# Moving blocks at a 1280-byte pitch, a shifted first weight tile, and smaller SSD buffers in an fp32 encoder kernel

## Chip, cores and metric

The kernel runs on one core of one Trainium2 chip. The metric is device time in microseconds (us) of one execution; several executions are timed and the median is quoted. One further execution is recorded by the hardware profiler, and all rows below come from that one.

## The reference, cut to what matters

Sixteen learned tokens are put ahead of 256 input tokens, so the sequence has L = 272 rows of D = 2048 channels. Layer 0 mixes tokens with a grouped 2-D Fourier transform, layer 1 with a bidirectional Mamba-2 mixer (SSD); each is followed by a SwiGLU channel mixer of width 5632. In layer 1 only the last 256 rows matter after the mixer.

```
h = concat(meta_tokens, x)                       # 272 x 2048
h = h + real(fft2(rms_norm(h))) @ fnet_w_out
h = h + (silu(u @ w_gate) * (u @ w_up)) @ w_down     # u = rms_norm(h)
h = h + ssd(rms_norm(h) @ w_in -> z, xBC, dt; conv of width 5 + silu on xBC) @ w_out
h = h + (silu(u @ w_gate) * (u @ w_up)) @ w_down
out = rms_norm(h)[16:]
```

## The kernel before, in words

All large products are taken as three fp32r matmuls, "high by high, high by low, low by high" (`mm3`, L108 to L110; the low part of the weights is L110). Every weight block comes from HBM as 1 MB in tile `w`; ScalarE rounds 1024 columns of it into `wh` (L101) and VectorE puts the rest into `wl` (L102), four buffers of each.

The stationary side of a matmul is 128 columns, 512 bytes a partition. The moving side is, in most products, a block of the normed input: `gh` (high) and `gl` (low) hold 16 blocks of 272 fp32 columns, and `gsl` picks block k. 272 columns are 1088 bytes, so block k begins 1088k bytes after the first: 64k bytes further each time if one counts modulo 256. `gh` itself begins at a multiple of 256, which a pad tile sees to. After the SSD mixer the same room is used as 16 blocks of 256 columns (`gh1`, `gl1`), 1024 bytes apart: each at a multiple of 256.

The helper `weights(..., place)` puts the split weights `place` elements into their buffer, whose size (4352 bytes) is a multiple of 256. The default is 16 elements, so the weights begin 64 bytes past a multiple of 256; `place` is 0 in the products in which the weights are the moving side, 512 columns wide (`w_z` in the SSD mixer and the down product of layer 1). There the stationary side is a slice of `gh` or of the hidden tile `hh`. `hh` and `hl` of layer 0 have blocks of 320 columns, 1280 bytes, of which 272 are used.

The order of the work is that of the program: in `swiglu` pieces of eight 128-column blocks of the hidden width; of each piece all gate and up products (`gemm_in`, 96 matmuls each, two PSUM tiles in turn), then the down product of the piece before. In layer 1 the pieces are 8, 8, 8, 8, 8, 2, 2 blocks: the gate and up products of the first two pieces stand one after the other (1536 matmuls, with `norm_scale` after the first 96), those of the later ones each follow a down product (768, 768, 768, 192, 192 matmuls).

In the SSD mixer eight head groups run through slots. A pair of groups begins with the B and the C products (`conv` on each, C with 258 columns that begin 56 bytes into a block), each group has two X products with `conv`, the `w_z` product, and then the output product of the group two back (`out_group`, L584; 48 matmuls for each of four q, moving side `yh`, `yl` at multiples of 256). `conv` is: L553 PSUM to `cu`, L559 ScalarE into `ca`, four L561 VectorE steps in `ca`, L563 SiLU into the destination. `to_tokens` transposes what `conv` made one slot later.

Two helpers are named in the steps below: `norm_scale` (one plain fp32 matmul, L172, then eleven VectorE steps into `rbc`) and `step_sizes` (the dt product and the decays).

Of the kernel before, what the change touches and what calls it, by code (L numbers as in the profile page):

```python
# [19 lines left out]
P = 128  # L20
D = 2048
# [19 lines left out]
XC, BC, CC = 0, DI, DI + G * NST  # L41
NRAW, NSP = 3, 4
RUN = 1024
LINE = 128
HC = 8
NEG = -1.0e30

# [2 lines left out]
def encoder(ctx: ExitStack, tc: tile.TileContext, I, out):  # L50
# [14 lines left out]
        return ptp.tile([P, 512], F32, tag="tp", name="tp")  # L65


    const.tile([P, LINE - 32], F32, name="pad")
    hT = const.tile([P, NB, L], F32, name="hT")
    gh = const.tile([P, NB, L], F32R, name="gh")  # L70
    gl = const.tile([P, NB, L], F32R, name="gl")
    ident = const.tile([P, P], F32, name="ident")
    ones = const.tile([P, P], F32, name="ones")
    cols = const.tile([P, 4 * P], F32, name="cols")

    def col(i):
        return cols[:, i : i + 1]
# [4 lines left out]
    def wffn(i, b):  # L82
        return col(32 + i * NB + b)

    def weights(src, k0, nk, c0, ncol, place=LINE // 8):

        w = wpool.tile([P, nk, ncol], F32, tag="w", name="w", bufs=NRAW)  # L90
        k1 = RUN // ncol
        nc.sync.dma_start(w.rearrange("p (u k) c -> p u (k c)", k=k1),
                          src[k0 // k1 : (k0 + nk) // k1, c0 // ncol].rearrange("u p x -> p u x"))
        parts = []
        n = min(nk, RUN // ncol)
        for k in range(0, nk, n):
            ks = slice(k, k + n)
            wh, wl = (wpool.tile([P, RUN + LINE // 2], F32R, tag=t, name=t, bufs=NSP)[:, place : place + n * ncol]
                      .rearrange("p (k c) -> p k c", c=ncol) for t in ("wh", "wl"))
            with tc.high_priority(offset=70):  # L100
                SC.copy(wh, w[:, ks, :])  # L101
                V.tensor_tensor(out=wl, in0=w[:, ks, :], in1=wh.bitcast(F32), op=ALU.subtract)  # L102
            parts.append((wh, wl))
        return parts
# [9 lines left out]
        return tuple(x[:, k % each, c0 : c0 + n] for x in u[k // each])  # L114


    gh1, gl1 = (x.rearrange("p b t -> p (b t)")[:, : NB * S].rearrange("p (b t) -> p b t", t=S) for x in (gh, gl))

    def gsl(k, a, b=L):
        if (a, b) == (NM, L):  # L120
            return gh1[:, k, :], gl1[:, k, :]
        return gh[:, k, a:b], gl[:, k, a:b]

    def gemm_in(src, c0, lo):

        n = L - lo
        pss = [mmtile(), mmtile()]
        for k0 in (0, 8):
            u = weights(src, k0, 8, c0, 256)
            for k in range(8):  # L130
                for j in range(2):
                    mm3(pss[j][:, :n], wsl(u, k, j * P), gsl(k0 + k, lo), k0 + k == 0, k0 + k == NB - 1)
        return pss
# [16 lines left out]
    ssq = npool.tile([P, L], F32, name="ssq")  # L150

    npool.tile([P, L], F32, tag="sq", name="sq", bufs=1)
    npool.tile([P, L], I32, tag="nyi", name="nyi")
    npool.tile([P, LINE // 2], F32, name="pad2")

    def norm_block(b, wcol, lo):

# [11 lines left out]
    def norm_scale(lo):  # L169

        ps = tptile()
        PE.matmul(ps[:, : L - lo], ones, ssq[:, lo:], start=True, stop=True)  # L172
        x = npool.tile([P, L], F32, tag="sq", name="nx", bufs=1)
        V.tensor_scalar(out=x[:, lo:], in0=ps[:, : L - lo], scalar1=1.0 / D, scalar2=EPS,
                        op0=ALU.mult, op1=ALU.add)
        yi = npool.tile([P, L], I32, tag="nyi", name="nyi")
        t = npool.tile([P, L], F32, tag="nyi", name="nt")
        y = rbc
        V.tensor_scalar(out=yi[:, lo:], in0=x[:, lo:].bitcast(I32), scalar1=1, scalar2=None,
                        op0=ALU.logical_shift_right)  # L180
        V.tensor_scalar(out=y[:, lo:].bitcast(I32), in0=yi[:, lo:], scalar1=-1.0, scalar2=float(0x5F3759DF),
                        op0=ALU.mult, op1=ALU.add)
        for it in range(3):
            V.tensor_tensor(out=t[:, lo:], in0=y[:, lo:], in1=y[:, lo:], op=ALU.mult)
            V.scalar_tensor_tensor(out=t[:, lo:], in0=t[:, lo:], scalar=-0.5, in1=x[:, lo:],
                                   op0=ALU.mult, op1=ALU.mult)
            V.scalar_tensor_tensor(out=y[:, lo:], in0=t[:, lo:], scalar=1.5, in1=y[:, lo:],
                                   op0=ALU.add, op1=ALU.mult)
# [4 lines left out]
    with ExitStack() as fx:  # L193
# [7 lines left out]
        ftl = early.tile([P, 2, 2, FD], F32R, name="ftl")  # L201
        fh = early.tile([P, NB, L], F32R, name="fh")
        fl = early.tile([P, NB, L], F32R, name="fl")
        tok = early.tile([P, 2, L], F32, name="tok")
        tokM = early.tile([KM, L], F32, name="tokM")
        tm3 = early.tile([KM, L], F32R, name="tm3")
        th = early.tile([P, 2, L], F32R, name="th")
        tl = early.tile([P, 2, L], F32R, name="tl")
# [12 lines left out]
        for q in range(4):  # L221
            nc.sync.dma_start(x[:, 1, q * 512 : (q + 1) * 512], xin[P : 2 * P, q * 512 : (q + 1) * 512])
        nc.sync.dma_start(rows, I["vectors"].rearrange("(i r) p -> r i p", r=P))
        nc.sync.dma_start(tok, I["c_tok"])
        nc.sync.dma_start(tokM, I["c_tokm"])
        nc.sync.dma_start(feat, I["c_feat"])

# [30 lines left out]

        def table(c, r):

            SC.activation(th[:, c, :], tok[:, c, :], AF.Identity, bias=0.0, scale=r)
            V.scalar_tensor_tensor(out=tl[:, c, :], in0=tok[:, c, :], scalar=r, in1=th[:, c, :].bitcast(F32),
                                   op0=ALU.mult, op1=ALU.subtract)

        with tc.manual_schedule():
# [8 lines left out]
            rA = rsqrt(early, ms3[:, 0:1], 1, "rA")  # L274
            residual(0, 0, pss[0])
            residual(0, 1, pss[1])
            SC.activation(gl.rearrange("p b t -> p (b t)")[:KM, :D], xm, AF.Square, accum_out=ssm[:KM])
            residual(0, 2, pss[2])
            residual(0, 3, pss[3])
            ps = mmtile()  # L280
# [16 lines left out]
            table(0, rA)  # L297
            rB = rsqrt(early, ms3[:, 1:3], 2, "rB")
            highM(quarters[0])
            SC.copy(cols, ps)  # L300
            residual(1, 2, pss[2])
            residual(1, 3, pss[3])
            table(1, rB[:, 0:1])
# [71 lines left out]
    def swiglu(layer, lo, tmp, pieces, down):  # L375
# [3 lines left out]
        for nf in pieces:  # L379

            hh = tmp.tile([P, HC, n + -n % 64], F32R, tag="hh", name="hh", bufs=2)[:, :, :n]
            hl = tmp.tile([P, HC, n + -n % 64], F32R, tag="hl", name="hl", bufs=2)[:, :, :n]
            for fp in range(nf // 2):
                c0 = (f0 + 2 * fp) * P
                s2 = []
                gate = gemm_in(wg, c0, lo)
                if c0 == 0:
                    norm_scale(lo)
                for ps in gate:
                    t1 = tmp.tile([P, n], F32, tag="t1", name="t1", bufs=2)  # L390
                    V.tensor_tensor(out=t1, in0=ps[:, :n], in1=rbc[:, lo:], op=ALU.mult)
                    s1 = tmp.tile([P, n], F32, tag="s1", name="s1", bufs=3)
                    SC.activation(s1, t1, AF.Silu)  # L393
                    GP.tensor_tensor(out=s1, in0=s1, in1=rbc[:, lo:], op=ALU.mult)  # L394
                    s2.append(s1)
                for j, ps in enumerate(gemm_in(wu, c0, lo)):
                    f = 2 * fp + j
                    t2 = tmp.tile([P, n], F32, tag="t2", name="t2", bufs=2)
                    V.tensor_tensor(out=t2, in0=ps[:, :n], in1=s2[j], op=ALU.mult)
                    SC.copy(hh[:, f, :], t2)  # L400
                    GP.tensor_tensor(out=hl[:, f, :], in0=t2, in1=hh[:, f, :].bitcast(F32), op=ALU.subtract)  # L401
            if pending is not None:
                down(*pending)
            pending = (f0, nf, hh, hl)
            f0 += nf
# [23 lines left out]
    with ExitStack() as fx:  # L429
# [2 lines left out]

        tm = sc0.tile([P, 5, P], F32, name="tm")
        tmM = sc0.tile([NM, H], F32, name="tmM")
        decA = sc0.tile([P, H], F32, name="decA")
        dsk = sc0.tile([P, H], F32, name="dsk")
        rtok = sc0.tile([P, 2 + 2 * 8], F32, name="rtok")[:, 0:2]
        scr = dram.tile([P, 2 * P], F32, name="scr")
# [28 lines left out]
        def step_sizes():  # L467
            u = weights(I["w_dt"], 0, NB, 0, P)
            ps = mmtile()
            for k in range(NB):  # L470
                mm3(ps[:, :L], wsl(u, k), gsl(k, 0), k == 0, k == NB - 1)
            norm_scale(0)


            pr = tptile()
            PE.matmul(pr[:, 0:1], ssq[:, CA[0] : CA[1]], ones[:, 0:1], start=True, stop=True)
            PE.matmul(pr[:, 1:2], ssq[:, CB[0] : CB[1]], ones[:, 0:1], start=True, stop=True)
            mst = sc0.tile([P, 2], F32, name="mst")
            V.tensor_scalar(out=mst, in0=pr[:, 0:2], scalar1=1.0 / D, scalar2=EPS, op0=ALU.mult, op1=ALU.add)
            rt = rsqrt(sc0, mst, 2, "rt")  # L480
# [68 lines left out]
        def conv(ps, blk, lo, dst):  # L549
# [1 line left out]
            n = L - lo  # L551
            u = so.tile([P, L], F32, tag="cu", name="cu", bufs=2)
            V.tensor_tensor(out=u[:, :n], in0=ps[:, :n], in1=rbc[:, lo:], op=ALU.mult)  # L553
            a = so.tile([P, L], F32, tag="ca", name="ca", bufs=2)

            def w(j):
                return col(114 + j * 48 + blk)
# [2 lines left out]
            for j, (o0, o1, i0) in ((0, (2, n, 0)), (1, (1, n, 0)), (3, (0, n - 1, 1)), (4, (0, n - 2, 2))):  # L560
                V.scalar_tensor_tensor(out=a[:, o0:o1], in0=u[:, i0 : i0 + o1 - o0], scalar=w(j),  # L561
                                       in1=a[:, o0:o1], op0=ALU.mult, op1=ALU.add)
            SC.activation(dst, a[:, :n], AF.Silu)  # L563

        def to_tokens(src, dst, dstM):

# [6 lines left out]

        def out_group(gi, q, yh, yl):

            u = weights(w_out, gi * 4, 4, q * 512, 512)
            for jp in range(2):
                pss = [mmtile(), mmtile()]
                for k in range(4):
# [145 lines left out]
        for gi in range(G):  # L725
            if gi % 2 == 0:

                bT = so.tile([P, 2, L], F32, tag="bT", name="bT", bufs=2)
                cT = so.tile([P, 2, S + 2], F32, tag="cT", name="cT", bufs=1)
                btok = sp.tile([P, 2, 2, P], F32, tag="btok", name="btok", bufs=2)  # L730
                btokM = sp.tile([NM, 2, P], F32, tag="btokM", name="btokM", bufs=2)
# [34 lines left out]
            pz = [mmtile(), mmtile()]  # L766
            for k in range(NB):
                if k % 4 == 0:
                    u = weights(I["w_z"], k, 4, gi * 512, 512, 0)
                for c, (a, b) in enumerate((CA, CB)):  # L770
                    mm3(pz[c], gsl(k, a, b), wsl(u, k % 4, 0, 512), k == 0, k == NB - 1)
            for c in range(2):
# [22 lines left out]
    with ExitStack() as fx:  # L795
# [2 lines left out]
        fw = tmp.tile([P, D], F32, name="fw")  # L798
        GP.dma_start(fw, I["norm_final_w"].partition_broadcast(P))
        sqj = tmp.tile([P, 512], F32, name="fsq")  # L800
        small = tmp.tile([P, LINE], F32, name="fsmall")
        sums = small[:, 0:8].rearrange("p (c q) -> p c q", c=2)
        ms = small[:, 8:10]

# [123 lines left out]
```

## Time and profile before

| what | us |
|---|---|
| median of three runs | 2446.23 (2445.91 to 2447.92) |
| the profiled execution, its own time | 2445.32 |
| its span, first to last instruction | 2443.5 |

The profiled execution is 0.9 us below the median. Matmuls overlap in the pipeline: each is listed with about 0.28 us, while the next one begins 0.113 to 0.125 us after it. The listed length is therefore not the cost; the step from start to start is. In a table of windows the count of a window also takes in the one to three matmuls that began ahead of it and still run at its left edge.

### The profile page before, as it was taken

The page shows a single profiled execution, that of the slowest core. Times are in us where ns is not written, and L with a number is a line of the kernel's source. Part 1 is how long each engine was busy: PE and PEld are TensorE (multiplying, and loading weights), DVE is VectorE, ACT ScalarE, POOL GpSimd, SP SyncE. Part 2 cuts the span into 40 slices and gives each one's busy share as a digit, 9 for nine tenths or more (in the row PEclk, how much of TensorE's full clock was granted, in tenths as well). Part 3 has the DMA queues.
Part 4 walks back from the last instruction along what each step waited for, and adds up shares of the span by engine and source line. Part 5 has one row for each costly group of instructions (what it writes and reads, how often), then busy time and mean ns, then how long its engine had stood idle before and what let it go on. Part 6 is the DMA issues. An engine that isn't in the chain of part 4 may idle for free.

```text
span 2443.5 us, 42924 instructions
## 1 busy us (share of the span) xinstructions
PE 2415.7 (99%) x17958; PEld 2305.0 (94%) x17958; DVE 1481.8 (61%) x2020; ACT 1212.1 (50%) x1784; POOL 407.6 (17%) x361
## 2 busy tenths in 40 slices
PE   8999999999999999999999999999999999999998
PEld 8999999999999999888989989989999998989887
DVE  7564544545454568778668768668554555555556
ACT  6444334343433346878557558445444443434334
POOL 3111111010101112231221221112221020202000
PEclk9999999999999999999999999999999999999999
DMA  5555555555555555655455555454655555555553
GB/s 165 175 177 180 175 173 175 181 179 174 174 179 181 175 173 175 216 174 189 164 179 193 180 173 184 162 173 161 202 191 186 191 184 192 184 194 184 190 192 132
DMA packets 115506, 438.66 MB, mean 180 GB/s; under 512 B 7360, under 2 KB 8080, under 8 KB 115136
## 3 DMA queue, kind: packets, MB, share of 16 engines
q1 hardware_dynamic: 110336, 417.86, 50.5%
q0 software_dynamic: 4832, 17.99, 2.3%
q8 instruction: 141, 2.31, 0.4%
q14 instruction: 53, 0.43, 0.0%
q10 hardware_dynamic: 144, 0.07, 0.0%
HBM read 433.66 MB, written 2.23 MB: 178 GB/s over the span
## 4 chain that ended last, share of the span: by engine, by line
PE 88%; DVE 4%; DMA 3%; issue 2%; ACT 2%; POOL 1%; SPq 0%; DVEq 0%; ACTq 0%; POOLq 0%
PE mm L109 28%; PE mm L110 28%; PE mm L108 28%; DMA pb<-scr 2%; DVE wl L102 1%; PE tp L659 1%; ACT wh L101 1%; DVE ca L561 1%; ACT pb L601 0%; DMA w<-fnet_w_out 0%; PE tp L643 0%; PE tp L682 0%; POOL pb L718 0%; PE tp L625 0%; PE tp L622 0%
## 5 line engine op out<-in xcount | busy, mean ns | idle before, releaser
L102 DVE TENSOR_TENSOR wl<-w,wh 128x1024 fp32r<-128x1024 f32 x786 | 971.1, 1237 | 833.3 <-ACT wh L101 830.2
L101 ACT CAST wh<-w 128x1024 fp32r<-128x1024 f32 x786 | 821.6, 1047 | 1085.6 <-PE mm L109 799.3
L109 PE MATMUL mm<-gl,wh 128*128 128x272 f32 (+2 forms) x3600 | 1027.0, 285 | 0.0
L110 PE MATMUL mm<-gh,wl 128*128 128x272 f32 (+2 forms) x3600 | 1024.3, 285 | 0.5 <-DVE wl L102 0.5
L108 PE MATMUL mm<-gh,wh 128*128 128x272 f32 (+2 forms) x3600 | 1021.8, 284 | 0.1
L109 PEld LDWEIGHTS mm<-gl,wh 128*128 128x128 f32 x3600 | 680.0, 189 | 0.8 <-issue 0.5
L108 PEld LDWEIGHTS mm<-gh,wh 128*128 128x128 f32 x3600 | 678.3, 188 | 1.1 <-issue 0.5
L110 PEld LDWEIGHTS mm<-gh,wl 128*128 128x128 f32 x3600 | 676.2, 188 | 0.9 <-DVE wl L102 0.7
L394 POOL TENSOR_TENSOR s<-s,rbc 128x272 f32<-128x272 f32 (+1 forms) x88 | 96.6, 1116 | 812.5 <-ACT s L393 812.5
L110 PE MATMUL mm<-hh,wl 128*128 128x272 f32 x704 | 201.8, 287 | 0.0
L109 PE MATMUL mm<-hl,wh 128*128 128x272 f32 x704 | 201.8, 287 | 0.0
L108 PE MATMUL mm<-hh,wh 128*128 128x272 f32 x704 | 201.8, 287 | 0.0
L401 POOL TENSOR_TENSOR hl<-t,hh 128x272 fp32r<-128x272 f32 (+1 forms) x88 | 97.0, 1120 | 395.4 <-ACT hh L400 395.4
L108 PE MATMUL mm<-yh,wh 128*128 128x256 f32 x512 | 145.5, 286 | 3.4 <-DVE hT L584 3.0
L109 PE MATMUL mm<-yl,wh 128*128 128x256 f32 x512 | 142.6, 279 | 0.5 <-DVE yl L688 0.5
L110 PE MATMUL mm<-yh,wl 128*128 128x256 f32 x512 | 142.5, 279 | 0.0
L108 PE MATMUL mm<-wh,hh 128*128 128x512 f32 x352 | 137.2, 390 | 0.0
L109 PE MATMUL mm<-wl,hh 128*128 128x512 f32 x352 | 137.1, 390 | 0.0
L110 PE MATMUL mm<-wh,hl 128*128 128x512 f32 x352 | 137.0, 389 | 0.0
L108 PEld LDWEIGHTS mm<-hh,wh 128*128 128x128 f32 x704 | 132.7, 188 | 0.0
L110 PEld LDWEIGHTS mm<-hh,wl 128*128 128x128 f32 x704 | 132.6, 188 | 0.0
L109 PEld LDWEIGHTS mm<-hl,wh 128*128 128x128 f32 x704 | 132.6, 188 | 0.0
(279 smaller groups left out, 2852.1 us busy)
## 6 DMA issues: line engine op xcount, KB each, us to landing
w<-ffn_w_gate SPq DMA_DIRECT2D x88, 1024.0 KB, 5.2
w<-ffn_w_up SPq DMA_DIRECT2D x88, 1024.0 KB, 5.1
w<-w_down SPq DMA_DIRECT2D x80, 1024.0 KB, 5.0
w<-w_xbc SPq DMA_DIRECT2D x48, 1024.0 KB, 5.3
w<-w_z SPq DMA_DIRECT2D x32, 1024.0 KB, 5.4
w<-ssd_w_out SPq DMA_DIRECT2D x32, 1024.0 KB, 5.0
w<-fnet_w_out SPq DMA_DIRECT2D x16, 1024.0 KB, 5.3
pb<-scr POOLq DMA_DIRECT2D x32, 512.0 KB, 5.6
```

Of the source, the lines that this page charges most:

```text
L101: SC.copy(wh, w[:, ks, :])
L102: V.tensor_tensor(out=wl, in0=w[:, ks, :], in1=wh.bitcast(F32), op=ALU.subtract)
L108: PE.matmul(ps, lhs[0], rhs[0], start=start, stop=False)
L109: PE.matmul(ps, lhs[0], rhs[1], start=False, stop=False)
L110: PE.matmul(ps, lhs[1], rhs[0], start=False, stop=stop)
L394: GP.tensor_tensor(out=s1, in0=s1, in1=rbc[:, lo:], op=ALU.mult)
L401: GP.tensor_tensor(out=hl[:, f, :], in0=t2, in1=hh[:, f, :].bitcast(F32), op=ALU.subtract)
L561: V.scalar_tensor_tensor(out=a[:, o0:o1], in0=u[:, i0 : i0 + o1 - o0], scalar=w(j), in1=a[:, o0:o1], op0=ALU.mult, op1=ALU.add)
L659: PE.matmul(py[:, e * HD : (e + 1) * HD], kern[c][:, e, :], xt[:, c, e * HD : (e + 1) * HD], start=True, stop=True)
```

## The change

Five things change. (1) `gh` and `gl` become one tile `g2` with blocks of 320 columns (`LP`), of which 272 are used; all 16 blocks begin at a multiple of 256 bytes. The 256-column form `gh1`, `gl1` stays packed at 1024 bytes, again at multiples of 256. Pads and tiles ahead of it are sized so that the starts of `g2`, `wh`, `wl`, the hidden tiles and the SSD tiles keep their place modulo 256. (2) The weights of `w_z` move from `place` 0 to 16. (3) A `first` argument: the first 1024-column part of the weights of some stretches of 256-column products begins at 0 instead of 64 bytes, which are the first gate product of every piece in layer 1 (24 matmuls) and the even q of `out_group` (the halves k = 0, 1 of its two column pairs). (4) `conv` works in place in its destination for the 272-column products; the C product keeps one `ca` buffer instead of two; `bT` has one buffer instead of two; `decA` lies in a free part of `tm`. (5) `norm_scale` uses `ssq` as its scratch, so the two small matmuls on `ssq` in `step_sizes` come ahead of it; the Fourier tables are loaded into `ssq`, the `sq` buffer and `rbc`, with two DMAs for `c_tok` instead of one; `cols` is 400 wide.

```diff
-LINE = 128
+LP = 320
+AT = 16
+NCOL = 400
...
-    gh = const.tile([P, NB, L], F32R, name="gh")
-    gl = const.tile([P, NB, L], F32R, name="gl")
+    g2 = const.tile([P, 2, NB, LP], F32R, name="g2")
+    gh, gl = g2[:, 0, :, :L], g2[:, 1, :, :L]
...
-    def weights(src, k0, nk, c0, ncol, place=LINE // 8):
+    def weights(src, k0, nk, c0, ncol, place=AT, first=None):
...
+            at = place if first is None or k else first
-            wh, wl = (wpool.tile([P, RUN + LINE // 2], F32R, tag=t, name=t, bufs=NSP)[:, place : place + n * ncol]
+            wh, wl = (wpool.tile([P, RUN + 64], F32R, tag=t, name=t, bufs=NSP)[:, at : at + n * ncol]
...
-    def gemm_in(src, c0, lo):
+    def gemm_in(src, c0, lo, first=AT):
-            u = weights(src, k0, 8, c0, 256)
+            u = weights(src, k0, 8, c0, 256, AT, None if k0 else first)
...
-        yi = npool.tile([P, L], I32, tag="nyi", name="nyi")
-        t = npool.tile([P, L], F32, tag="nyi", name="nt")
-        y = rbc
+        yi, t, y = ssq.bitcast(I32), ssq, rbc
...
-        nc.sync.dma_start(tok, I["c_tok"])
+        for c in range(2):
+            nc.sync.dma_start(tok[c], I["c_tok"][:, c])
...
-                gate = gemm_in(wg, c0, lo)
+                gate = gemm_in(wg, c0, lo, 0 if lo and fp == 0 else AT)
...
-        decA = sc0.tile([P, H], F32, name="decA")
+        decA = tm[:, 4, H:]
...
-            norm_scale(0)
             pr = tptile()
             PE.matmul(pr[:, 0:1], ssq[:, CA[0] : CA[1]], ones[:, 0:1], start=True, stop=True)
             PE.matmul(pr[:, 1:2], ssq[:, CB[0] : CB[1]], ones[:, 0:1], start=True, stop=True)
+            norm_scale(0)
...
-            a = so.tile([P, L], F32, tag="ca", name="ca", bufs=2)
+            a = dst if lo == 0 else so.tile([P, S + 2], F32, tag="ca", name="ca", bufs=1)
-            SC.activation(dst, a[:, :n], AF.Silu)
+            SC.activation(dst, a, AF.Silu)
...
-            u = weights(w_out, gi * 4, 4, q * 512, 512)
+            u = weights(w_out, gi * 4, 4, q * 512, 512, AT, None if q % 2 else 0)
...
-                bT = so.tile([P, 2, L], F32, tag="bT", name="bT", bufs=2)
+                bT = so.tile([P, 2, L], F32, tag="bT", name="bT", bufs=1)
...
-                    u = weights(I["w_z"], k, 4, gi * 512, 512, 0)
+                    u = weights(I["w_z"], k, 4, gi * 512, 512)
```

## Rows read from the trace of the kernel before

**Rows 1.** Page: the span, and the first line of busy time by engine.

```profile
span 2443.5 us, 42924 instructions
...
PE 2415.7 (99%) x17958; PEld 2305.0 (94%) x17958; DVE 1481.8 (61%) x2020; ACT 1212.1 (50%) x1784; POOL 407.6 (17%) x361
```

**Rows 2.** Waits of PE: what waited, for whom, us in total, times, longest.

```profile
PE tp L240 <- DMA ident<-c_ident: 5.2, 1, 5.2
PE mm L108 <- DVE hT L584: 3.0, 4, 1.2
```

**Rows 3.** Groups of PE's instructions, shapes kept apart: count, then busy us, mean ns.

```profile
L108 PE MATMUL mm<-gh,wh 128*128 128x272 f32 x2064 | 591.5, 287 | 0.0
L108 PE MATMUL mm<-gh,wh 128*128 128x256 f32 x1408 | 393.7, 280 | 0.1
...
L108 PE MATMUL mm<-yh,wh 128*128 128x256 f32 x512 | 145.5, 286 | 3.4 <-DVE hT L584 3.0 <-ACT yh L687 0.5
...
L108 PE MATMUL mm<-wh,gh 128*128 128x512 f32 x256 | 101.6, 397 | 0.0
...
L108 PE MATMUL mm<-gh,wh 128*128 128x258 f32 x128 | 36.6, 286 | 0.0
```

**Rows 4.** Windows of stretches: us, PE busy (matmuls), granted clock, DMA share, GB/s.

```profile
309.63:405.63 96.00, 96.00 (x770) 1.00 0.51 176
405.63:452.99 47.36, 47.36 (x386) 1.00 0.55 179
1720.00:1820.00 100.00, 100.00 (x885) 1.00 0.59 198
2010.39:2053.93 43.54, 43.54 (x194) 1.00 0.56 190
2053.93:2144.39 90.46, 90.46 (x770) 1.00 0.57 188
```

**Rows 5.** Windows inside two stretches of the output product (first, second of a group).

```profile
1347.00:1356.00 9.00, 9.00 (x82) 1.00 0.33 117
1361.00:1370.00 9.00, 9.00 (x79) 1.00 0.39 123
```

**Rows 6.** Timeline, PE, from a down product to the next gate product, layer 1.

```profile
2053.71 0.39 PE L110 MATMUL mm<-wh,hl 128*128 128x512 f32 x1
2053.93 0.28 PE L108 MATMUL mm<-gh,wh 128*128 128x256 f32 x1
2054.05 0.28 PE L109 MATMUL mm<-gl,wh 128*128 128x256 f32 x1
```

**Rows 7.** Timeline, PE, around the plain fp32 matmul of `norm_scale` in layer 1.

```profile
1708.70 0.60 PE L172 MATMUL tp<-ssq,ones 128*128 128x256 f32 x2
1708.94 0.47 PE L108 MATMUL mm<-gh,wh 128*128 128x256 f32 x1
```

**Rows 8.** Timeline, PE, beginning of a down product of layer 1.

```profile
2010.39 0.40 PE L108 MATMUL mm<-wh,hh 128*128 128x512 f32 x1
...
2011.55 0.39 PE L110 MATMUL mm<-wh,hl 128*128 128x512 f32 x1
...
2012.23 0.39 PE L110 MATMUL mm<-wh,hl 128*128 128x512 f32 x1
```

**Rows 9.** Timeline, PE: first matmul of a `w_z` product, first instruction behind it.

```profile
1323.18 0.48 PE L108 MATMUL mm<-wh,gh 128*128 128x512 f32 x1
...
1345.51 0.27 PE L568 MATMUL tp<-ident,xs 128*128 128x128 f32 x1
```

**Rows 10.** Groups of instructions, all engines, from 940 to 1700 us (SSD).

```profile
L561 DVE SCALAR_TENSOR_TENSOR ca<-cu,cols,ca 128x270 f32<-128x270 f32 (+3 forms) x192 | 86.4, 511 | 0.3 <-ACT ca L559 0.2
...
L563 ACT ACT_TABLE_LOAD x23 | 29.5, 1283 | 13.1 <-DVE ca L561 12.6
L559 ACT ACTIVATE ca<-cu,cols 128x272 f32<-128x272 f32 (+1 forms) x48 | 27.1, 606 | 11.3 <-DVE cu L553 11.2
```

**Rows 11.** The instructions that touch tile `tok`: the DMA issue.

```profile
L224 SPq DMA_DIRECT2D tok<-c_tok x1: 339/339/339, 9.8 to 9.8; - x1
```

More of the change, by code (lines that the diff above doesn't have):

```diff
@@ L65, in tptile @@
         return ptp.tile([P, 512], F32, tag="tp", name="tp")
-    const.tile([P, LINE - 32], F32, name="pad")
+    cols = const.tile([P, NCOL], F32, name="cols")
+    const.tile([P, 16], F32, name="pad")
     hT = const.tile([P, NB, L], F32, name="hT")
-    gh = const.tile([P, NB, L], F32R, name="gh")
-    gl = const.tile([P, NB, L], F32R, name="gl")
+    g2 = const.tile([P, 2, NB, LP], F32R, name="g2")
+    gh, gl = g2[:, 0, :, :L], g2[:, 1, :, :L]
     ident = const.tile([P, P], F32, name="ident")
     ones = const.tile([P, P], F32, name="ones")
-    cols = const.tile([P, 4 * P], F32, name="cols")
     def col(i):
@@ L114, in wsl @@
         return tuple(x[:, k % each, c0 : c0 + n] for x in u[k // each])
-    gh1, gl1 = (x.rearrange("p b t -> p (b t)")[:, : NB * S].rearrange("p (b t) -> p b t", t=S) for x in (gh, gl))
+    gh1, gl1 = (g2[:, i].rearrange("p b t -> p (b t)")[:, : NB * S].rearrange("p (b t) -> p b t", t=S)
+                for i in range(2))
     def gsl(k, a, b=L):
@@ L152, in encoder @@
     npool.tile([P, L], F32, tag="sq", name="sq", bufs=1)
-    npool.tile([P, L], I32, tag="nyi", name="nyi")
-    npool.tile([P, LINE // 2], F32, name="pad2")
+    npool.tile([P, 16], F32, name="pad")
     def norm_block(b, wcol, lo):
@@ L203, in encoder @@
         fl = early.tile([P, NB, L], F32R, name="fl")
-        tok = early.tile([P, 2, L], F32, name="tok")
-        tokM = early.tile([KM, L], F32, name="tokM")
+        tok = (ssq, npool.tile([P, L], F32, tag="sq", name="tok1", bufs=1))
+        tokM = rbc[:KM]
         tm3 = early.tile([KM, L], F32R, name="tm3")
@@ L259, in table @@
         def table(c, r):
-            SC.activation(th[:, c, :], tok[:, c, :], AF.Identity, bias=0.0, scale=r)
-            V.scalar_tensor_tensor(out=tl[:, c, :], in0=tok[:, c, :], scalar=r, in1=th[:, c, :].bitcast(F32),
+            SC.activation(th[:, c, :], tok[c], AF.Identity, bias=0.0, scale=r)
+            V.scalar_tensor_tensor(out=tl[:, c, :], in0=tok[c], scalar=r, in1=th[:, c, :].bitcast(F32),
                                    op0=ALU.mult, op1=ALU.subtract)
@@ L276, in encoder @@
             residual(0, 1, pss[1])
-            SC.activation(gl.rearrange("p b t -> p (b t)")[:KM, :D], xm, AF.Square, accum_out=ssm[:KM])
+            SC.activation(g2[:KM, 1].rearrange("p b t -> p (b t)")[:, :D], xm, AF.Square, accum_out=ssm[:KM])
             residual(0, 2, pss[2])
@@ L299, in encoder @@
             highM(quarters[0])
-            SC.copy(cols, ps)
+            SC.copy(cols, ps[:, :NCOL])
             residual(1, 2, pss[2])
@@ L800, in encoder @@
         sqj = tmp.tile([P, 512], F32, name="fsq")
-        small = tmp.tile([P, LINE], F32, name="fsmall")
+        small = tmp.tile([P, 128], F32, name="fsmall")
         sums = small[:, 0:8].rearrange("p (c q) -> p c q", c=2)
```

## The prediction, made before the changed kernel ran

> **What bounds the kernel now.** I read the page first: PE is busy for 99% of the span and its weight loads for 94%, while the next engine, DVE, is at 61% [rows 1]. Then the waits of PE, longest first after the start of the program: the costliest is 3.0 us in all, against 5.2 for the first load [rows 2]. So the time is the sum of PE's steps from one matmul to the next, and nothing that DVE, ACT or the DMAs save would be seen. The table of PE's instructions then says how many steps there are of each width [rows 3]; each row there is one of the three lines of `mm3`, so the counts go times three: 6192 matmuls of 272 columns on `gh`, 4224 of 256 on the packed form, 1536 of 256 on `yh`, 768 of 512 in `w_z`, 384 of 258. A mean of 276 to 290 ns in that table is not a step, because matmuls overlap. So the next view is that of windows that are cut at the first matmul of a stretch and the first behind it. Their length by the program's count of matmuls is the step, and here the kernel shows what the change is about: the same work goes at different steps, with the granted clock at 1.00 (the level of 2.4 GHz) in all of them [rows 4].
>
> - Gate and up of layer 0, blocks 1088 bytes apart, so that their starts move by 64 bytes modulo 256: 96.00 us by 768 matmuls, 125.0 ns.
> - Down of layer 0, the same 272 columns, the same weights at 64, but blocks 1280 bytes apart: 47.36 by 384, 123.3 ns.
> - Gate and up of layer 1, 256 columns: within the first long stretch 100.00 us hold 885 matmuls less the two or three that reach in from the left, 113.3 ns; in the stretch after a down product 90.46 by 768, 117.8 ns. The places of the operands are the same in both; only what came before differs.
> - The output products show the same two steps: windows of 9.00 us hold 82 or 79 [rows 5].
>
> The 256-column product thus has two patterns, a short step and a long step, and keeps the one in which it begins. Each of the five stretches that follow a down product has the long step; the long stretch before them has the short one, and it begins behind a plain fp32 matmul [rows 7].
>
> **The change part by part.** *Pitch of 1280 bytes.* After it, a 272-column product on `gh` has moving blocks at multiples of 256 and weights at 64: the arrangement of the down product of layer 0, down to the pitch. I take its step: 125.0 - 123.3 = 1.67 ns, times 6192 = **-10.3 us** [rows 3, 4]. The bounds are nothing and that. The 384 matmuls of C begin 56 bytes into a block before and after; no row has them with all blocks alike, so between nothing and the same 1.67 ns, 0.6 us; I take 0.
>
> *First weights at 0, gate products.* Of the 4224 gate and up matmuls of layer 1, the pieces behind a down product have 3 x 768 + 2 x 192 = 2688, all at 117.8. If the new beginning leaves them at the short step, that is 4.5 ns x 2688 = **-12.0 us** [rows 3, 4]. Is it likely? Where both operands begin at a multiple of 256, as in the down product of layer 1, the first five steps take 1.16 us (2010.39 to 2011.55), 232 ns each, and the next three 0.68, 227 each [rows 8], and the whole stretch averages 43.54 by 192, 226.8, twice 113.4 [rows 4]. So equal places pull a long-step beginning into the short step. The 24 matmuls with weights at 0 are four times as many as that took. What follows has the weights at 64, where a short step lasts for at least the 880 matmuls of its window. Against it stands the handover in [rows 6]: the down product has the short step (2053.71 to 2053.93, 0.22 us), the very next gate product with weights at 64 the long one at once (0.12). There the width changes together with the place; in the changed kernel the place alone changes, 24 matmuls on. I take that the short step survives it, by a small margin; the other end is nothing.
>
> *First weights at 0, output products.* Seven of the fourteen stretches of 96 and most of the last 288 have the long step, some 870 of 1536 matmuls; the short one in all of them would be -3.9 us [rows 3, 5]. But within an even q the place goes 0, 64, 0, 64, so the handover has to hold three times; I take **-2 us**, between nothing and -3.9.
>
> *`w_z` at 64.* Before, weights of `gh` at 64, 128, 192, 0 in turn meet a moving side at 0: 22.33 us from 1323.18 to 1345.51 for 96 matmuls, 232.6 ns [rows 9]. After, both sides begin at 64. The nearest row with equal places is the down product's 226.8 [rows 4]: 5.8 x 768 = -4.5 us at most, nothing at least. The beginning of each of the eight stretches, behind transposes, remains, and places equal at 64 are not places equal at 0: **-3 us**.
>
> *Smaller SSD buffers.* The conv in place has the same instructions; its destination is taken some steps sooner, and `xs` has four buffers of which two are freed a slot earlier. `bT`'s last reader is in the second group of a pair, ahead of that group's `w_z` and output products, so the next pair's conv finds it free. Only the C product changes its order: with one `ca`, the ScalarE step L559 of the second block waits for the SiLU of the first. Queued behind it on ACT are the roundings into `wh`, and PE waits for those if four buffers run out. The delay is a table load of 1.28, a SiLU, and L559's own 0.6; with the SiLU taken like L559 that is 2.5 us, four times, **+10 us at most** if PE stood through all of it, nothing at least [rows 10]. PE hardly waits for these chains now [rows 2], so I take **+2 us**.
>
> *The rest.* One more issue of 0.34 us on SP's queue, ahead of the feature table and the first weights [rows 11]: +0.3 at most, and I take it. `norm_scale` behind two one-column matmuls, `ssq` as its scratch and `cols` cut to 400 add no instruction. The first writer of `ssq` afterwards comes a whole product later.
>
> Sum: -10.3 - 12.0 - 2 - 3 + 2 + 0.3 = -25.0 us. Against the profiled execution's 2445.3 this is 2420.3; the median of the runs lies 0.9 above that execution, which gives **2421 us**.
>
> **The rivals.**
> *The shifted beginning does nothing*: each stretch keeps the step that it has now. For it speaks [rows 6], where going from place 0 to 64 ended in the long step. Then -10.3 - 3 + 2.3 = -11.0: 2435 us.
>
> *It ends in the long step everywhere.* The second piece's shifted weights come in the middle of the long short-step stretch; if going from 0 to 64 always ends so, its 768 matmuls take the long step, and so do the other 666 of the output products: 1434 x 4.5 = +6.4 us, so -4.6 in all: 2441.6 us.
>
> *The places have no effect at all, and the two steps have another cause.* Then only the +2.3 of waits and the DMA is left: 2448.5 us. Against it: the two products of layer 0 differ in pitch alone and differ in step [rows 4]. The Trainium skill has the rule behind this rival, on the page "TensorE: Matmul & The Clock Gate", Part 2, on loading weights: PE reads weights and moving data through two independent ports, and loading the next weights takes no read bandwidth from a running matmul. The trace doesn't agree with the reading that nothing but width counts: one width has two steps here, 113.3 and 117.8 ns.
>
> *Slower: equal blocks lock the 272-column products into a long step.* With the turning starts of today every matmul meets another arrangement, and the mean is 125.0 whatever came before. With all blocks alike, a stretch may hold on to a bad beginning, as the 256-column ones do. If the long step costs the same 4.5 ns there, the step is 123.3 + 4.5 = 127.8, +2.8 x 6192 = +17.3 us, and the shifted beginnings don't help by the same stubbornness: +17.3 - 3 + 2.3 = +16.6: 2463 us. It decides the sign once the mean step is above 125.0. Against it: the down product of layer 0 has all its blocks alike, and its step is 123.3 straight behind a gate product whose steps vary [rows 4].
>
> **How the numbers follow.** Chances: the forecast 0.50; beginning does nothing 0.27; ends long 0.12; no effect 0.05; lock 0.06. With the bounds of the output products, `w_z` and the waits, the likeliest case alone reaches from 2415 (-30.7) to 2429 (the full +10). The range takes in the second case and most of the third, 2414 to 2440. A difference of 0.2%, 4.9 us, is about what these runs can tell from none, so faster means below 2441.3: the first two cases and half of the third, 0.83. The same: the other half and the case without effect, 0.11. Slower: 0.06.
>
> **What would show each step.** Windows over gate and up of layer 0: 768 matmuls in 94.7 us instead of 96.0; if 96.0, the pitch does nothing, if above, it locks. Windows over the gate stretches behind a down product: 87.0 us for 768 at the short step, 90.5 at the long one; the timeline of their first 30 matmuls shows which step the 24 at place 0 have and what the 25th starts. The middle of the long first stretch: 882 in 100 us, or 849 from the second piece on. `w_z` from start to end: 21.9 instead of 22.33. PE's waits between 940 and 1700 us: new entries of 1 to 2 us at the C products if one `ca` buffer is felt. The prediction is wrong by more than its range if the 272-column step is above 125, or if the shifted beginning turns short steps into long ones while waits in the SSD mixer eat the rest.

## The result and the profile after

The changed kernel takes 2460.70 us (median of four runs, 2458.66 to 2463.22); the kernel before took 2447.07 beside it (2445.91 to 2448.03). The ratio is 1.0056, with an interval of 1.0039 to 1.0074: slower by 14 us, where 25 less were forecast. The profiled execution took 2463.22 us, the longest of the four and 2.5 above their median.

The first line and the first busy line of the page after, which answer to [rows 1]:

```profile
span 2461.4 us, 42918 instructions
...
PE 2419.7 (98%) x17958; PEld 2310.2 (94%) x17958; DVE 1487.1 (60%) x2020; ACT 1228.0 (50%) x1796; POOL 400.4 (16%) x361
```

The span grew by 17.9 us. PE has the same 17958 instructions; ACT has 12 more than before.

Windows of PE in the changed kernel (us, busy and matmuls, granted clock, DMA share, GB/s): gate and up of layer 0; a first `w_z` product; in the long gate stretch of layer 1, what follows the first 24 matmuls of the first piece there, to its end, and what follows the 24 shifted ones of the second piece; a gate stretch behind a down product.

```profile
307.58:402.30 94.72, 94.72 (x771) 1.00 0.52 177
982.30:1004.19 21.89, 21.89 (x100) 1.00 0.60 196
1726.02:1799.46 73.44, 73.44 (x651) 1.00 0.59 196
1802.33:1889.96 87.63, 87.63 (x746) 1.00 0.56 188
1937.52:2028.02 90.50, 90.50 (x770) 1.00 0.55 188
```

768 matmuls of 272 columns take 94.72 us, 123.3 ns each, against 96.00 in [rows 4]; 96 of `w_z` take 21.89 against 22.33 in [rows 9]. Both are the forecast values. The gate stretch behind a down product is still at 90.50, the long step. The beginning of such a stretch, timeline of PE:

```profile
1937.29 0.39 PE L113 MATMUL mm<-wh,hl 128*128 128x512 f32 x1
1937.52 0.28 PE L111 MATMUL mm<-g,wh 128*128 128x256 f32 x1
1937.63 0.28 PE L112 MATMUL mm<-g,wh 128*128 128x256 f32 x1
1937.75 0.28 PE L113 MATMUL mm<-g,wl 128*128 128x256 f32 x1
...
1940.27 0.28 PE L113 MATMUL mm<-g,wl 128*128 128x256 f32 x1
1940.38 0.28 PE L111 MATMUL mm<-g,wh 128*128 128x256 f32 x1
```

The first matmul at place 0 has a step of 0.11 us, as the short step would; the other 23, from 1937.63 to 1940.38, take 2.75 us, 119.6 each. That is a third step, longer than the long one. The 25th, whose weights are at 64 again, starts the long step. In the long first stretch the second piece's shifted weights turn the short step into the long one for the rest: ahead of them 648 matmuls take 73.44 us, 113.3 ns each, and behind them 744 take 87.63, 117.8 each.

The waits of PE from 900 to 1700 us (what waited, for whom, us in total, times, longest):

```profile
PE tp L572 <- DVE yl L692: 9.2, 2, 5.3
PE tp L572 <- DVE yb L657: 4.3, 1, 4.3
PE mm L113 <- DVE wl L105: 2.0, 2, 1.3
```

Before, the costliest of PE's waits after the program's start was 3.0 us in all [rows 2]. Here the transposes (L572) stand three times for 4 to 5 us until a `tp` buffer has been read. Around the wait that ends at 1327.92 the granted clock falls, and PE runs at half clock for a while: from 1329.05 the 512-column steps are 427 ns, and the window 1329.05 to 1333.74 has a granted clock of 0.50 (1.2 GHz) before it returns to 2.4. The mixer has four such stretches; the first begins behind a wait of 1.3 us, the others lie around the three waits for `tp`. The first row is the window just named, the rest are the four:

```profile
1329.05:1333.74 4.69, 4.69 (x12) 0.50 0.67 235
1016.58:1020.00 3.42, 3.42 (x17) 0.50 0.77 237
1098.50:1105.33 6.83, 4.17 (x20) 0.50 0.87 327
1327.20:1334.02 6.82, 6.10 (x16) 0.50 0.77 277
1521.76:1528.58 6.82, 4.61 (x13) 0.50 0.69 210
```

Added up from start to start, 272-column steps give -10.1 us and `w_z` steps -3.3 (both without the steps that a wait or the half clock lengthens); the 256-column gate and up products cost +3.7 (491.4 to 495.1) and the output products +3.5 (186.8 to 190.3). Of the +17.9 that leaves about +24, in the SSD mixer: waits and the half clock behind them. PE's waits from 900 to 1700 us are 22.0 in all against 8.4 before, +13.6. In the four windows PE is busy for 18.3 us at half clock; with steps of 427 ns instead of 227 some 9 us of that are lost (an estimate from these rows). By the medians, 13.6 us apart, the mixer's share would be about 20.

### The profile page after: what moved, and what is told of

It reads as the page before. It is cut to its first block, busy times and chain, and to the rows that moved or that the text cites. A ratio compares the mean times of both kernels' runs of the same rounds, so it can differ in the third digit from the quotient of the medians.

```text
span 2461.4 us, 42918 instructions
## 1 busy us (share of the span) xinstructions
PE 2419.7 (98%) x17958; PEld 2310.2 (94%) x17958; DVE 1487.1 (60%) x2020; ACT 1228.0 (50%) x1796; POOL 400.4 (16%) x361
## 4 chain that ended last, share of the span: by engine, by line
PE 85%; DVE 5%; issue 3%; ACT 3%; DMA 2%; POOL 1%; SPq 0%; DVEq 0%; ACTq 0%; POOLq 0%
PE mm L112 27%; PE mm L111 27%; PE mm L113 27%; DMA pb<-scr 2%; DVE wl L105 2%; ACT wh L104 1%; PE tp L663 1%; ACT pb L605 1%; DVE xs L565 0%; POOL pb L722 0%; PE tp L686 0%; PE tp L647 0%; DVE pb L607 0%; DVE bT L565 0%; ACT L567 0%
## 5 line engine op out<-in xcount | busy, mean ns | idle before, releaser
L111 PE MATMUL mm<-g,wh 128*128 128x272 f32 (+2 forms) x3600 | 1026.1, 285 | 0.5 <-ACT wh L104 0.4
L113 PE MATMUL mm<-g,wl 128*128 128x272 f32 (+2 forms) x3600 | 1023.3, 284 | 2.0 <-DVE wl L105 2.0
L112 PE MATMUL mm<-g,wh 128*128 128x272 f32 (+2 forms) x3600 | 1022.9, 284 | 0.0
L111 PEld LDWEIGHTS mm<-g,wh 128*128 128x128 f32 x3600 | 683.1, 190 | 1.8 <-ACT wh L104 1.1
L113 PEld LDWEIGHTS mm<-g,wl 128*128 128x128 f32 x3600 | 678.1, 188 | 2.7 <-DVE wl L105 2.5
L112 PEld LDWEIGHTS mm<-g,wh 128*128 128x128 f32 x3600 | 678.2, 188 | 0.8 <-issue 0.5
```

Source lines behind the costliest of these rows:

```text
L111: PE.matmul(ps, lhs[0], rhs[0], start=start, stop=False)
L112: PE.matmul(ps, lhs[0], rhs[1], start=False, stop=False)
L113: PE.matmul(ps, lhs[1], rhs[0], start=False, stop=stop)
```

## The experiments

"Beside" is the kernel before on the same chips. Where a median has no count, it is that of one run.

**The shifted beginnings taken out.**

```diff
-                gate = gemm_in(wg, c0, lo, 0 if lo and fp == 0 else AT)
+                gate = gemm_in(wg, c0, lo)
...
-            u = weights(w_out, gi * 4, 4, q * 512, 512, AT, None if q % 2 else 0)
+            u = weights(w_out, gi * 4, 4, q * 512, 512)
```

> The changed kernel with all weights of 256-column products at 64 bytes again. If the shifted beginnings cause long steps (0.120 us for the matmuls at place 0, 0.118 behind them): the second piece of gate and up in layer 1 returns to 0.1133 us a matmul and about half of the output products too, together 7 us less than the changed kernel, about 2453.5 us; the stalls in the SSD mixer stay. Rival, the two steps are chance that any edit ahead redraws: some stretches change step, others not, and the time is anywhere from 2446 to 2460.

2452.72 us (7 runs), beside 2446.34; 1.0028 [1.0017, 1.0039], 8.0 below the changed kernel. Windows of the second piece in the long stretch and of a stretch behind a down product:

```profile
1794.18:1881.23 87.05, 87.05 (x771) 1.00 0.59 195
1928.79:2019.24 90.45, 90.45 (x769) 1.00 0.57 188
```

The long stretch keeps the short step through the whole second piece, to its end, while the stretches behind a down product have the long one with or without the shift. The shift only costs.

**C in place as well**, so that no `ca` is left in the changed kernel.

```diff
-            a = dst if lo == 0 else so.tile([P, S + 2], F32, tag="ca", name="ca", bufs=1)
+            a = dst
```

> The changed kernel with the C product's conv in place in its destination too, so that no single ca buffer is left for its two blocks to wait for. Theory (one ca buffer delays the second block, and ScalarE and VectorE run late behind it): the stalls of 1.6 to 5.7 us of PE behind the C products go, some 20 us less than the changed kernel, about 2441. Rival (conv in place for the B and X products, or the one bT buffer, makes the stalls): they stay, 2460. Second rival (PE now runs ahead because its steps are shorter): they stay, 2460.

2446.62 (10 runs), beside 2446.34; 1.0000 [0.9991, 1.0010]: 14.1 below the changed kernel. The waits of PE in the mixer:

```profile
PE mm L111 <- DVE hT L588: 5.0, 6, 2.0
PE tp L572 <- DVE yb L657: 2.8, 1, 2.8
```

The 9.2 us for `yl` are gone; some waits that the kernel before does not have remain (there `hT` has 3.0 in all [rows 2]), so the kernel is slower than was expected. The mean granted clock of the profiled execution is 0.998, as in the kernel before; in the changed kernel, and in the one without the shift, it is 0.994.

**The smaller SSD buffers alone**, in the kernel before.

```diff
-            a = so.tile([P, L], F32, tag="ca", name="ca", bufs=2)
+            a = dst if lo == 0 else so.tile([P, S + 2], F32, tag="ca", name="ca", bufs=1)
...
-                bT = so.tile([P, 2, L], F32, tag="bT", name="bT", bufs=2)
+                bT = so.tile([P, 2, L], F32, tag="bT", name="bT", bufs=1)
```

> The kernel before with the smaller conv and bT buffers alone: conv in place for 272 columns, one ca buffer for C, one bT. Theory of the single ca buffer: stalls behind the C products as in the changed kernel, 2446 plus 15 to 22 us, about 2465. Rival (the stalls come from PE's shorter steps): no stalls, 2446.

2464.27 (4 runs), beside 2446.34; 1.0078 [1.0061, 1.0095]. This part alone costs 17.9 us, and the mean granted clock is 0.994 here too. Waits of PE in the mixer:

```profile
PE tp L568 <- DVE yl L688: 5.9, 2, 3.3
PE tp L568 <- DVE yb L653: 3.4, 1, 3.4
PE tp L622 <- POOL xtM L618: 2.9, 1, 2.9
```

**The X and B convs in place, with two `ca` for C and two `bT`**, in the kernel before.

```diff
-            a = so.tile([P, L], F32, tag="ca", name="ca", bufs=2)
+            a = dst if lo == 0 else so.tile([P, S + 2], F32, tag="ca", name="ca", bufs=2)
...
-            SC.activation(dst, a[:, :n], AF.Silu)
+            SC.activation(dst, a, AF.Silu)
```

> The kernel before with conv in place for the 272-column products, but two ca buffers for C and two bT. Theory of the single ca buffer: as before, 2446 within 3 us. Rival (conv in place makes the stalls, since the destination is held from the first step on): about 2460.

2448.90 (10 runs), beside 2446.34; 1.0012 [1.0003, 1.0022]: +2.6.

**The same with one `bT`.**

```diff
-                bT = so.tile([P, 2, L], F32, tag="bT", name="bT", bufs=2)
+                bT = so.tile([P, 2, L], F32, tag="bT", name="bT", bufs=1)
```

> The kernel before with conv in place for 272 columns and two ca buffers for C, as in the run of that alone (2448.9), and one bT instead of two. Theory (the single ca buffer makes the stalls, bT is free when it is needed): 2449. Rival (bT is the buffer that is waited for): 2464, as with both.

2449.43 (10 runs), beside 2445.88; 1.0015 [1.0005, 1.0024], not to be told from the last. What is left between this kernel and the smaller buffers alone is one `ca` instead of two: 2464.27 - 2449.43 = 14.8 us (14.4 if each is taken against the kernel before beside it).

**No shift and C in place**, the two edits from above together in the changed kernel.

> The changed kernel without the shifted beginnings and with the C product's conv in place. If the two costs found so far are separate, their gains add: 2446.6 less 7 to 8 is 2439. Rival (the stalls that are left in the SSD mixer move when the steps change): 2436 to 2446.

2439.59 (10 runs), beside 2445.88; 0.9973 [0.9963, 0.9983].

**`w_z` back at place 0 in that kernel.**

```diff
-                    u = weights(I["w_z"], k, 4, gi * 512, 512)
+                    u = weights(I["w_z"], k, 4, gi * 512, 512, 0)
```

> The kernel without shifted beginnings and with C in place, but the weights of w_z at place 0 as before the change, against blocks of the normed input that now all begin at 64 bytes past a multiple of 256. Theory (equal places make the short step in the 512-column product): the steps go back from 227 to 231 or 233 ns, 3 to 4.5 us more, about 2442.5. Rival (it was the turning of the block starts, and the pitch alone cures it): no difference, 2439.

2442.02 (10 runs), beside 2445.88; 0.9983 [0.9973, 0.9992], 2.4 above the last. The first `w_z` product, from its start to its end, here:

```profile
982.17:1004.66 22.49, 22.49 (x99) 1.00 0.69 220
```

and in the kernel with `w_z` at 64:

```profile
982.23:1004.10 21.87, 21.87 (x100) 1.00 0.65 214
```

Eight times this difference is 5.0 us, more than the 2.4 between the medians. The profiled execution with `w_z` at 0 has no half-clock stretch in the mixer, and the one with `w_z` at 64 has 6.8 us of it; that can be a part of the rest, which no run here takes apart.

**A plain fp32 matmul ahead of each gate stretch behind a down product**, as the long stretch has one ahead of it [rows 7], in the kernel without shift and with C in place (2439.59). So are the edits that follow.

```diff
+                if lo and fp == 0 and f0 >= 16:
+                    pr = tptile()
+                    PE.matmul(pr[:, :n], ones, ssq[:, lo:], start=True, stop=True)
                 gate = gemm_in(wg, c0, lo)
```

> The kernel of the run before with one plain fp32 matmul of 256 columns (as in norm_scale, its result unused) ahead of the gate product of the five pieces that follow a down product in layer 1. Theory (the beginning decides, and behind a plain fp32 matmul the 256-column stretch begins in the short step): these 2688 matmuls go from 117.8 to 113.3 ns, 12.0 us less, five extra matmuls cost some 0.5 us each: 9 to 10 us less than without, about 2429.5. Rival (the first stretch has the short step for another reason, such as what DMA or ScalarE do at that time): no gain, 2.5 us more, 2441.5.

2430.50 (4 runs), beside 2445.88; 0.9939 [0.9924, 0.9954]. The first of these stretches has the short step, behind a longer first one:

```profile
1915.31:2002.55 87.24, 87.24 (x770) 1.00 0.57 193
```

**One column instead of 256 in it.**

```diff
-                    PE.matmul(pr[:, :n], ones, ssq[:, lo:], start=True, stop=True)
+                    PE.matmul(pr[:, :1], ones, ssq[:, lo : lo + 1], start=True, stop=True)
```

> As the run with the plain fp32 matmul ahead of five gate products (2430.5), but with one column instead of 256. Theory (any plain fp32 matmul breaks the pattern of weight load and product, and the short step follows): the same 113.3 ns, and the five cost less, 2429 to 2430. Rival (the pause of some 0.2 us that the 256 columns make is what counts): 117.8 ns again, about 2439.5.

2428.89 (4 runs), beside 2446.21; 0.9929 [0.9914, 0.9944].

**An fp32r matmul with both sides at a multiple of 256 bytes** instead of the plain fp32 one; its product is not used.

```diff
-                    PE.matmul(pr[:, :n], ones, ssq[:, lo:], start=True, stop=True)
+                    PE.matmul(pr[:, :n], gh1[:, 0, :P], gh1[:, 0, :], start=True, stop=True)
```

> As the run with the plain fp32 matmul, but the extra matmul is fp32r, on 128 columns of the normed input against 256 of it, result unused. Theory (it takes a plain fp32 matmul, behind which the next weights are loaded apart from a running product): the stretches stay at 117.8 ns, about 2440. Rival (any matmul with other places in between does it): 113.3 ns, about 2429.

2427.14 (4 runs), beside 2446.21; 0.9924 [0.9907, 0.9940]: the lowest median of all, ahead of both kernels, though four runs each don't tell it from the one-column matmul. The theory that it must be plain fp32 fell. Timeline of PE at the boundary:

```profile
1913.44 0.39 PE L113 MATMUL mm<-wh,hl 128*128 128x512 f32 x1
1913.67 0.28 PE L392 MATMUL tp<-g 128*128 128x256 f32 x1
1913.78 0.28 PE L111 MATMUL mm<-g,wh 128*128 128x256 f32 x1
1913.89 0.28 PE L112 MATMUL mm<-g,wh 128*128 128x256 f32 x1
```

and the window of the stretch behind it:

```profile
1913.78:2000.82 87.04, 87.04 (x771) 1.00 0.57 194
```

**The same matmul with its weights at 64 bytes.**

```diff
-                    PE.matmul(pr[:, :n], gh1[:, 0, :P], gh1[:, 0, :], start=True, stop=True)
+                    PE.matmul(pr[:, :n], gh1[:, 0, AT : AT + P], gh1[:, 0, :], start=True, stop=True)
```

> As the run with one extra fp32r matmul ahead of five gate products (2427.1), but with its weights 64 bytes past a multiple of 256, like those that follow. Theory (a single matmul at another place is what shifts the beginning into the short step): no change of place, so 117.8 ns and about 2440. Rival (one matmul more is enough, whatever its place): 113.3 ns, about 2427.

2439.39 (8 runs), beside 2446.38; 0.9973 [0.9962, 0.9984]: nothing gained. The same stretch:

```profile
1915.08:2005.53 90.45, 90.45 (x770) 1.00 0.57 188
```

So of the fp32r matmul it is the place that counts, and not that there is one matmul more.

**Six at place 0 instead of one.**

```diff
-                    PE.matmul(pr[:, :n], gh1[:, 0, :P], gh1[:, 0, :], start=True, stop=True)
+                    for r in range(6):
+                        PE.matmul(pr[:, :n], gh1[:, r, :P], gh1[:, r, :], start=r == 0, stop=r == 5)
```

> As the run with one extra fp32r matmul at place 0, but with six of them on end. In the changed kernel the 24 matmuls at place 0 begin with a step of 114, go to 120, and 117.8 follows. Theory (equal places in a 256-column product have a long step of their own, 120, and whoever leaves it is in the long step): the later ones of the six step at 120, then 117.8, about 2441. Rival (an extra matmul ahead is what counts, however many): 113.3 behind them, about 2430.

2442.98 (8 runs), beside 2446.38; 0.9986 [0.9975, 0.9998]. Here the six take from 1915.92 to 1916.63, 0.71 us, and the stretch has the long step:

```profile
1915.92 0.87 PE L393 MATMUL tp<-g 128*128 128x256 f32 x6
1916.63 0.28 PE L111 MATMUL mm<-g,wh 128*128 128x256 f32 x1
```

The window of the stretch:

```profile
1916.63:2007.09 90.46, 90.46 (x771) 1.00 0.54 185
```

**Two, three, four and seven**, by the same edit, one run each, beside one of 2443.24.

> Two extra 256-column matmuls at place 0 ahead of each of the five gate products behind a down product. Theory 'one only': whatever comes after the first matmul at place 0 runs with a step of 120 ns, and the handover out of that always ends in the long step, so 768 gate and up matmuls take 90.5 us, 117.8 ns each; time about 2441. Rival 'odd and even': an odd number at place 0 hands over into the short step and an even one into the long step, as one did and six and 24 did not: 90.5 us here as well, but 87.1 with three. Rival 'a few are allowed': 87.1 us, 113.3 ns; time about 2428.

> Three instead of two. 'One only': 90.5 us for 768, time about 2442. 'Odd and even': 87.1 us, time about 2429. 'A few are allowed': 87.1 us if two had it too.

> Four. 'One only' and 'odd and even': 90.5 us for 768, time about 2442. 'A few are allowed': 87.1 if the limit lies above four.

> Seven. 'One only' and 'a few are allowed': 90.5 us for 768, since six had it, time about 2444. 'Odd and even': 87.1 us, time about 2431.

2439.62, 2444.05, 2445.83 and 2442.77 us. Windows of the first gate stretch behind a down product, with two:

```profile
1913.37:2003.83 90.46, 90.46 (x771) 1.00 0.56 187
```

with three:

```profile
1917.28:2007.74 90.46, 90.46 (x771) 1.00 0.55 187
```

All four take 90.46 us, whether the number is odd or even. The windows decide here; single times that lie 6 us apart do not. "One only" holds: a single matmul at place 0 hands over into the short step; two, three, four, six, seven and the 24 of the changed kernel into the long one.

## Why the prediction was wrong, point by point

*Pitch of 1280 bytes: right.* -10.1 us from the steps against -10.3; 123.3 ns from the first stretch to the last, so the slower rival, a lock in a long step, is excluded.

*`w_z` at 64: right.* -3.3 from the steps against -3; with `w_z` alone put back, 2.4 us between the medians and 5.0 by the windows of the first product.

*First weights at 0, gate and output products: the step that failed.* The prediction took it that "equal places pull a long-step beginning into the short step", from the 512-column rows [rows 8], and that more matmuls at place 0 only make that surer. In a 256-column product the first matmul at place 0 has 0.11 us and every further one 119.6 ns, and the handover to place 64 then ends in 117.8. The experiments with one against two, three, four, six and seven show it: the 24 were not "four times as many as that took" but 23 too many. What came is the rival "it ends in the long step everywhere": +7.2 us by the steps, +8.0 between the medians with and without the shift, where that rival had +6.4. [rows 6] spoke for it and was waved off because the width changed there too. (One count in the term is off: fourteen stretches of 96 and a last of 288 are more than 1536. The trace before has fourteen of 96 and one of 192, with some 830 long steps instead of 870; the bound of 3.9 would be 3.7.) The -12.0 of the gate term could be had: one matmul at place 0 ahead of each of the five stretches takes 2439.59 to 2427.14, 12.45 us for 2688 matmuls, 4.6 ns each.

The reading that places have no effect, which the prediction weighed, is contradicted further: moving the weights of one matmul by 64 bytes turns 87.04 us into 90.45. The Trainium skill ("TensorE: Matmul & The Clock Gate", "Step-by-step: what each phase is for") says that loading the next weights takes no read bandwidth from the running matmul. That rule alone doesn't give these steps; whether the two reads meet somewhere, no run here shows.

*Smaller SSD buffers: mis-sized.* The term was +2 with +10 as its upper bound; alone it measured +17.9, of which one `ca` for C is 14.8. Its working counted the second block's delay on ACT (2.5 us a pair), and of what is queued behind it only the roundings into `wh`. It put the further table loads, the late `yh` and `yl`, and the half clock behind the waits at nothing. That `bT` would be free was right: one `bT` instead of two costs nothing that can be told. Timeline of ACT in the changed kernel (rows left out between):

```profile
1303.12 1.28 ACT L567 ACT_TABLE_LOAD   x1
1304.41 0.42 ACT L567 ACTIVATE cT<-ca 128x258 f32<-128x258 f32 x1
1304.85 1.28 ACT L605 ACT_TABLE_LOAD   x1
...
1306.45 0.59 ACT L563 ACTIVATE ca<-cu,cols 128x258 f32<-128x258 f32 x1
...
1311.53 1.28 ACT L567 ACT_TABLE_LOAD   x1 [0.77 <-DVE cu L556]
1312.82 0.42 ACT L567 ACTIVATE cT<-ca 128x258 f32<-128x258 f32 x1
...
1320.40 0.40 ACT L605 ACTIVATE pb<-pb,tm 128x128 f32<-128x128 f32 x1 [1.56 <-POOL pb L722]
1320.83 1.28 ACT L567 ACT_TABLE_LOAD   x1
1322.12 0.43 ACT L567 ACTIVATE xs<-xs 128x272 f32<-128x272 f32 x1
...
1325.48 1.28 ACT L605 ACT_TABLE_LOAD   x1
1326.78 0.40 ACT L605 ACTIVATE pb<-pb,tm 128x128 f32<-128x128 f32 x1
1327.08 0.61 ACT L691 ACTIVATE yh<-tp,cols 128x128 fp32r<-128x128 f32 x2
```

The same place in the kernel before:

```profile
1303.38 1.28 ACT L563 ACT_TABLE_LOAD   x1
1304.68 0.73 ACT L563 ACTIVATE cT<-ca 128x258 f32<-128x258 f32 x2
```

Timeline of PE at the end of that chain:

```profile
1323.61 0.39 PE L112 MATMUL mm<-wl,g 128*128 128x512 f32 x1
1327.92 0.48 PE L572 MATMUL tp<-ident,xs 128*128 128x128 f32 x1 [3.92 <-DVE yl L692]
```

With two buffers the SiLUs of both C blocks stand together behind one table load (one entry of two at 1304.68). With one, the second block's first step waits for the first SiLU and its own SiLU comes at 1312.82, with an exponential's table between. From 1303 to 1327 us ACT has six table loads where the kernel before has four, and the exponentials (L605), which themselves wait for POOL, now stand ahead of `xs` and of `yh`. So `yh` and `yl` empty their `tp` buffers about 5 us later and PE stands at its next transposes; the half clock goes with it. The whole program has 71 table loads against 59 before; with the smaller buffers alone also 71, with C in place 57, and with two `ca` and one `bT` 57 as well. The 12 more are the 12 further ACT instructions of the page, and 12 x 1.283 = 15.4 us of ACT. What the experiments show is that the single `ca` is the cause; the way from it to PE is read from these traces, not tried step by step.

The Trainium skill ("ScalarE: Activation LUTs", "What ACT_TABLE_LOAD costs") gives about 1283 ns for the load and a drain of some 1380 more for each switch of sets. The trace agrees with the first (1283 in [rows 10]); of the second it shows nothing: the load at 1303.12 begins 0.02 us after the exponential ahead of it ends, and the SiLU follows at its end.

*The two misses together.* With the shift alone gone wrong, the prediction's own sum ends at about 2442; with the buffers alone at 17.9 instead of 2 it ends at about 2437, within its range. Its last sentence names the two together as what would break the range, but gave them no price and no chance of their own.

*The rest.* That the order of `step_sizes` and the split DMA cost nothing more was not tried by itself. Without shift and `ca`, 2439.59 is 6.3 below before where the two right terms give 13.4; about 7 us stay in the mixer: waits (5.3 for `hT` and 3.1 for `yb` in that kernel, 3.0 and 0.8 before) and two half-clock stretches, 6.8 us in all, which cost about half of that by the rows above (an estimate). The in-place convs show 2.6 of it in the kernel before; the source of the rest stays open.

## What to carry to other kernels

A step measured in one stretch holds for another only if the width, the places and what ran just before are all the same: read it at the boundary, and try the boundary alone. A buffer count of two on a chain that shares ScalarE also keeps two activations of one table side by side, so before it is cut to one, follow what queues behind the second activation down to PE's next transpose. A table of parts that are changed one at a time is worth its runs: here two parts gave what was forecast, and two others took more than that back.

## What the runs showed of the hardware that was not expected

- 256 fp32r columns have three steps at the same granted clock: 113.3, 117.8 and 119.6 ns. The last belongs to weights and moving side both at a multiple of 256 bytes, from the second matmul on; the first two to weights at 64, by what ran before. One matmul at place 0, 0.11 us, decides for the 768 that follow. Why one gives the short step and two give the long one is open; no run here shows the cause.
- Three kinds of restart gave the short step: a plain fp32 matmul of 256 columns (-9.1 us), of one column (-10.7) or an fp32r one at place 0 (-12.45), each between its median and 2439.59.
- Around a PE wait of 3.92 us the granted clock fell to 0.50; from 1329.05 to 1333.74 the 512-column step was 427 ns instead of 227. Four such stretches cost some 9 us (an estimate), so one `ca` less is paid for twice, in waits and in clock.
